# A four-layer decoder trunk on one core: q and k computed transposed, rotated by a partition shuffle, and scored two heads at a time

## The chip, the cores and the metric

The kernel runs on one core of a Trainium2 chip. The metric is the device time of one execution in microseconds, the median of several runs. The core has a matrix engine (TensorE, PE in the profile; its weight loads are PEld), a vector engine (VectorE, DVE), an activation engine (ScalarE, ACT), a general engine (GpSimd, POOL) and a queue for DMAs (SyncE, SP).

## The reference

The input is one sequence of 256 tokens with 1024 features in fp32. Four layers follow each other. Each has a token mixer and a SwiGLU FFN (1024 to 2 x 2816 to 1024), and after each of the two `x <- LN(alpha * x + f(x))`. The mixers are causal attention with heads of 64; the first 16 dims of each head of q and k are rotated by position (dims 0 to 7 with 8 to 15).

- Layers 0 and 3: 16 query heads, 4 key and value heads, a window of 128 keys, a learned sink per head in the softmax, biases on q, k, v and the output.
- Layer 1: three groups of q, k, v with windows and strides (128, 1), (512, 4) and (2048, 16), 16 heads each. The groups' outputs are merged by their softmax denominators, which is one softmax over all three groups' keys.
- Layer 2: block-sparse attention with blocks of 256. With 256 tokens no past block exists, so it is causal attention within the block, 16 heads.

```python
def apply_rope(x, cos, sin):                       # x1, x2: dims 0-7 and 8-15 of each head
    return concatenate([x1 * c - x2 * s, x2 * c + x1 * s, x[..., 16:]])
s = einsum('bnqhgd,bnkhd->bnhgqk', qb, kb) * dh ** -0.5   # masked, softmax, times v
x = layer_norm(DN_ALPHA * x + mixer(x), ln_g[i, 0], ln_b[i, 0])
x = layer_norm(DN_ALPHA * x + swiglu(x), ln_g[i, 1], ln_b[i, 1])
```

## The kernel before

**Numbers in two parts.** Every fp32 operand of a product is kept as two fp16 parts, high and low. `mm3` (L127 to L132) issues three matmuls for one product: high x high (L130), high x low (L131), low x high (L132). Weights come from DRAM in fp32, in chunks of 1024 x 512 (128 partitions x 8 k-tiles x 512 columns). `load_w` casts each chunk in pieces of 1024 columns: ACT writes the high part `whi` (L91), DVE the low part `wlo` (L92). Four chunks fit in SBUF at a time, so casts run ahead of their use by that much. `split` (L134 to L139) makes the two parts of an activation: ACT the high one (L135), DVE the low one (L137 or L139).

**Projections.** `proj` (L178) computes 128 tokens x 512 columns of `x @ w` with the transposed activations `xth`, `xtl` as the stationary operand and the weights moving, 24 matmuls of 512 columns. For q and k the result has tokens on partitions. It is copied to the tile `qkv` (by ACT at L520, or with its bias by DVE at L455), rotated in place on POOL by four instructions on the 16 rotated dims of each head (L197 to L200, `rope`), transposed by PE with four fp32 transposes of 128 x 128 (L206), and split into `qkh`, `qkl` (L135, L137). Those hold two heads on the 128 partitions, 64 dims each. The transposes wait in a list `late` and are issued 8 projection steps later, or earlier where `flush` asks for them. For layers 0 and 3 the 4 key heads are first copied twice side by side (L466), so that a key head lies on the same 64 partitions as each query head that uses it.

**Attention.** `attend` (L212) makes steps for a list of items. An item is one query tile of 128 tokens with two heads (layers 0, 2, 3) or one head and its three key groups (layer 1). The step `scores` issues `mm3` on 64 partitions per head and key group, takes mask and row maximum on DVE straight from PSUM (L252) and the exponential with its row sum on ACT (L255). `flip` transposes the probabilities on PE (L268) and splits them, `values` multiplies by v into the tile `pv`, `collect` transposes the normalised output (L299). They are issued 0, 2, 3 and 4 items later. PSUM has 8 banks: three accumulators `acc`, four tiles `at` for scores and transposes, one `pv`.

**Order.** `weave` issues the attention steps of one set of heads evenly between the projection steps of the next set; `finish` does the same with the output projection of the heads that are done, and ends with the layer norm. The framework then puts the instructions in order at build time, by the program's order and by its own estimate of when operands are ready, so the order on an engine can differ from the program's. It also writes all waits. Each engine works through its queue in order.

Of the kernel before, what the change touches and what calls it, by code (L numbers as in the profile page):

```python
# [32 lines left out]
# Weights are scaled by a power of two before they are split into two fp16  # L33
# parts, so that the low part stays in fp16's normal range.
# [9 lines left out]
def trunk(ctx, tc, a, out):  # L44
# [16 lines left out]
    cc = const.tile([P, NT, ROT], F32, name="cc")  # L61
    ss = const.tile([P, NT, ROT], F32, name="ss")
    h8 = ROT // 2
# [32 lines left out]
    def weight_list():  # L96
        for li in range(DEPTH):
            kind, j = li % 3, li // 3
            if kind == 0:
                for c in (2, 0, 1):  # L100
                    yield a["w_a"][j, c], 8
                wo_ = a["w_ao"][j]
            else:
                m, wo_ = (a["w_b"], a["w_bo"][0]) if kind == 1 else (a["w_c"], a["w_co"][0])
                for c in range(m.shape[0]):
                    yield m[c], 8
            for h in range(2):
                yield wo_[h], 8
            for c in range(NFB // 2):
                yield a["w_gu"][li, c], 8  # L110
            for h in range(2):
                for c, n in enumerate((8, 8, 6)):
                    yield a["w_dn"][li, h, :, 4096 * c:4096 * c + 512 * n], n
# [30 lines left out]
    def weave(main, fill):  # L144
        """issue two lists of steps, evenly interleaved"""
# [9 lines left out]
    def transpose_x(t, XT, half):  # L155
        """columns of X[t] (512 of them) -> XT, in two parts"""
# [10 lines left out]
    late, age = [], [0]  # L167

    def flush(keys=None):
        """issue the transposes that wait: all, or those up to the last that writes one of keys"""  # L170
        while late and (keys is None or any(e[1] in keys for e in late)):
            late.pop(0)[2]()

    def proj(XT, w, t, evac):
        """steps for [128 tokens, 512] = x @ w for a chunk of 512 columns"""
        cell = {}

        def k_step(k):  # L178
            if k == 0:
                cell["ps"] = acc.tile([P, 512], F32, name="acc")  # L180
            mm3(cell["ps"], sl2(XT, ALL, k, tok(t)), sl2(w, ALL, k), k == 0, k == NK - 1)
            age[0] += 1
            while late and age[0] - late[0][0] >= LAG:
                late.pop(0)[2]()
            if k == NK - 1:
                evac(cell["ps"], t)
        return [lambda k=k: k_step(k) for k in range(NK)]

    def rope(y, t, nh):
        """y [128, nh, 64] fp32, in place"""  # L190
        t1 = sm.tile([P, nh, ROT], F32, name="rope1", bufs=2)
        t2 = sm.tile([P, nh, ROT], F32, name="rope2", bufs=2)
        cb = cc[:, t:t + 1, :].to_broadcast([P, nh, ROT])
        sb0 = ss[:, t:t + 1, :h8].to_broadcast([P, nh, h8])
        sb1 = ss[:, t:t + 1, h8:].to_broadcast([P, nh, h8])
        e = nc.gpsimd
        e.tensor_tensor(t1, y[:, :, :ROT], cb, op=OP.mult)  # L197
        e.tensor_tensor(t2[:, :, :h8], y[:, :, h8:ROT], sb0, op=OP.mult)
        e.tensor_tensor(t2[:, :, h8:], y[:, :, :h8], sb1, op=OP.mult)
        e.tensor_tensor(y[:, :, :ROT], t1, t2, op=OP.add)  # L200

    def transpose_qk(y, t, dst):
        """y [128 tokens, 4 pairs of heads x 128] -> dst parts [128, 4, 256 tokens]"""
        ps = ats.tile([P, 4, P], F32, name="at")
        for j in range(4):
            nc.tensor.transpose(ps[:, j], y[:, j * P:(j + 1) * P], ident)  # L206
        split(dst[0][:, :, tok(t)], dst[1][:, :, tok(t)], ps)
# [4 lines left out]
    def attend(items, oT):  # L212
        """steps for softmax attention. items: (query tile, heads, keys of their transposes), with heads [(head, groups, sinks)]
        and groups [(qT, kT, v)]: qT, kT parts [64, 256], v parts [128, NT, 64]; sinks [128, heads]
        (negated) or None. The groups' keys share one softmax. Four heads in a row, of one query tile,
        make a quad, whose outputs are normalised and transposed together."""
        st, quads = {}, {}

        def quad(i):
            t, heads = items[i][:2]  # L220
            return quads.setdefault((t, heads[0][0] // 4), {})

        def scores(i):
            t, heads = items[i][:2]
            flush([(k, tt) for k in items[i][2] for tt in range(t + 1)])
            nk, ng, nh = (t + 1) * P, len(heads[0][1]), len(heads)
            per, n = 512 // nk, nk * ng
            sk, mk = heads[0][2], MASK[heads[0][3]][t]
# [3 lines left out]
            s = sm.tile([P, 768], F32, name="s", bufs=4)  # L232
            s = s[:, :nh * (n + (sk is not None))].rearrange("p (h n) -> p h n", h=nh)
            if sk is not None:
                nc.gpsimd.tensor_copy(s[:, :, n], sk)
            mn = sm.tile([P, 4], F32, name="mn", bufs=6)
            ps = None
            for hi, (h, groups, _, _) in enumerate(heads):
                m = None
                for g, (qT, kT, _) in enumerate(groups):  # L240
                    u = hi * ng + g
                    if u % per == 0:
                        ps = ats.tile([P, 512], F32, name="at")
                    o = u % per * nk
                    mm3(ps[:, o:o + nk], sl2(qT, ALL, tok(t)), sl2(kT, ALL, slice(0, nk)), True, True)
                    if u % per == per - 1 or g == ng - 1:
                        # the groups of this head in this bank
                        g0 = max(0, g - u % per)
                        c0, c1 = g0 * nk, (g + 1) * nk
                        init = (3e38 if sk is None else sk[:, hi:hi + 1]) if m is None else m  # L250
                        m = mn[:, 2 * hi + (g0 > 0):2 * hi + (g0 > 0) + 1]
                        nc.vector.tensor_tensor_reduce(  # L252
                            s[:, hi, c0:c1], ps[:, o + nk - (c1 - c0):o + nk], mk[:, c0:c1], scale=-QSC,
                            scalar=init, op0=OP.add, op1=OP.min, accum_out=m)
                nc.scalar.activation(s[:, hi], s[:, hi], AF.Exp, bias=m, scale=-1.0,  # L255
                                     accum_out=q["l"][:, h % 4:h % 4 + 1])
            st[i] = s

        def flip(i):
            t, heads = items[i][:2]  # L260
            nq = len(heads[0][1]) * (t + 1)
            nb = len(heads) * nq
            s, parts = st[i], []
            for b0 in range(0, nb, 4):
                bn = min(4, nb - b0)
                ps = ats.tile([P, 4, P], F32, name="at")
                for b in range(bn):
                    nc.tensor.transpose(ps[:, b], s[:, (b0 + b) // nq, tok((b0 + b) % nq)], ident)  # L268
# [6 lines left out]
        def values(i):  # L275
            t, heads = items[i][:2]
# [4 lines left out]
            for h, groups, _, _ in heads:  # L281
                nb = len(groups) * (t + 1)
                for b in range(nb):
                    g, kt = divmod(b, t + 1)
                    mm3(q["o"][:, h % 4], parts.pop(0), sl2(groups[g][2], ALL, kt), b == 0, b == nb - 1)
            if h % 4 == 3:
# [4 lines left out]
        def collect(i):  # L291
            t, heads = items[i][:2]
            h, q = heads[-1][0], quad(i)
            if h % 4 != 3:
                return
# [4 lines left out]
            pr = slice(h // 4 * 2, h // 4 * 2 + 2)  # L300
            split(oT[0][:, pr, tok(t)], oT[1][:, pr, tok(t)], ps)
# [8 lines left out]
    def halves(tq, pr, hh):  # L310
        return sl2(tq, slice(hh * DH, (hh + 1) * DH), pr)
# [43 lines left out]
    def out_steps(PS, lhs, nk, w, h, t, ks, k0=0):  # L355
        """steps of PS[h, t] += lhs.T @ w over the k-tiles ks (of w's, w starting at k0)"""
# [67 lines left out]
    def finish(li, oT, items, kA, folded=False):  # L424
        """the last heads' attention, beside the output projection of the others, and LN"""
# [6 lines left out]
        f0 = o(0, range(kA))  # L432
        weave(attend(i0, oT), f0[:5] + [flush] + f0[5:])
# [8 lines left out]
    def mixer_a(li, j, XT):  # L442
        bias = hbuf("hth")[:, :1536]
# [4 lines left out]
        vv = (big.tile([P, NT, 4, DH], F16, name="avh"), big.tile([P, NT, 4, DH], F16, name="avl"))  # L448
# [3 lines left out]
        def evac(c):  # L452
            def fn(ps, t):
                y = two.tile([P, 512], F32, name="qkv", bufs=3)
                nc.vector.scalar_tensor_tensor(y, ps, 1.0 / WS, bias[:, 512 * c:512 * c + 512],  # L455
                                               op0=OP.mult, op1=OP.add)
                yh = y.rearrange("p (h d) -> p h d", d=DH)
                if c < 2:
                    rope(yh, t, 8)
# [260 lines left out]
```

## Time and profile before

| | |
|---|---|
| Time, median of 3 runs | 1289.69 us (1289.64 to 1290.55) |
| Span of the profiled execution | 1288.2 us; its own time is not given beside the span |
| PE busy | 1265.8 us |
| DVE busy | 873.0 us |
| ACT busy | 664.0 us |
| POOL busy | 112.7 us |
| DMA | 233.31 MB, mean 181 GB/s |
| Granted TensorE clock, mean | 0.997 of full |

A span runs from the first to the last instruction of one execution. "Busy" is the time in which at least one instruction of an engine was under way. Matmuls overlap in their pipeline, so the duration of one is longer than the distance to the next; that distance, read from a timeline of starts, is what a matmul costs in a full queue. In a timeline, consecutive instructions of one line and kind are merged into one row, with their count behind an x.

### The profile page before, as it was taken

What the parts mean: (1) busy time and instruction counts of PE and PEld (TensorE: products, weight loads), DVE (VectorE), ACT (ScalarE), POOL (GpSimd) and SP (SyncE); (2) the same over time, 40 slices, a digit from 0 to 9 for tenths busy, and PEclk for the clock granted to TensorE, in tenths of its full rate; (3) what the DMA queues carried; (4) which work ended last, traced back from release to release, by engine and by line L of the source; (5) the groups of instructions that cost most, each with busy time, mean ns of one, the idle gap of its engine ahead of it and who ended that gap; (6) DMA issues with size and microseconds to landing.
All of it is one profiled execution on the core that took longest, in us unless ns stands there. A gap on an engine that the chain in (4) does not pass through costs nothing. (4 is left out here: it accounts for less than half of the span.)

```text
span 1288.2 us, 24678 instructions
## 1 busy us (share of the span) xinstructions
PE 1265.8 (98%) x10352; PEld 844.9 (66%) x10352; DVE 873.0 (68%) x1451; ACT 664.0 (52%) x1117; POOL 112.7 (9%) x230
## 2 busy tenths in 40 slices
PE   7989999999999999999999999999999999999997
PEld 3549988444555555589884445589884445898843
DVE  5888766475565666777665667777665687876652
ACT  5765654345555565446544456536544366464430
POOL 1410000012011101000000020100000041000000
PEclk9999999999999999999999999999999999999999
DMA  8445755656345334347555564247555552475520
GB/s 316 166 164 197 263 200 184 221 206 222 145 147 173 139 131 151 112 163 251 209 181 180 201 225 162 100 164 257 203 180 182 223 207 99 153 250 207 190 87 33
DMA packets 35663, 233.31 MB, mean 181 GB/s; under 512 B 4448, under 2 KB 4448, under 8 KB 9696
## 3 DMA queue, kind: packets, MB, share of 16 engines
q1 hardware_dynamic: 35552, 231.74, 51.0%
q8 instruction: 81, 1.33, 0.4%
q14 instruction: 30, 0.25, 0.1%
HBM read 230.68 MB, written 1.05 MB: 180 GB/s over the span
## 5 line engine op out<-in xcount | busy, mean ns | idle before, releaser
L92 DVE SCALAR_TENSOR_TENSOR wlo<-raw,whi 128x1024 f16<-128x1024 f32 x416 | 500.3, 1223 | 206.1 <-ACT whi L91 205.8
L91 ACT ACTIVATE whi<-raw 128x1024 f16<-128x1024 f32 x416 | 414.6, 1049 | 258.9 <-PE acc L132 92.1
L131 PE MATMUL acc<-xtl,whi 128*128 128x256 f16 (+1 forms) x1792 | 408.2, 250 | 0.0
L132 PE MATMUL acc<-xth,wlo 128*128 128x256 f16 (+1 forms) x1792 | 408.2, 250 | 0.0
L130 PE MATMUL acc<-xth,whi 128*128 128x256 f16 (+1 forms) x1792 | 408.0, 250 | 0.1
L130 PE MATMUL acc<-whi,xth 128*128 128x512 f16 x480 | 183.3, 382 | 2.4 <-ACT xth L135 2.4
L131 PEld LDWEIGHTS <-whi 128*128 128x128 f16 x1792 | 175.3, 98 | 12.5 <-issue 0.3
L130 PEld LDWEIGHTS <-whi 128*128 128x128 f16 x1792 | 175.3, 98 | 11.9
L131 PE MATMUL acc<-wlo,xth 128*128 128x512 f16 x480 | 183.0, 381 | 0.2 <-DVE wlo L92 0.2
L132 PE MATMUL acc<-whi,xtl 128*128 128x512 f16 x480 | 182.8, 381 | 0.3
L132 PEld LDWEIGHTS <-wlo 128*128 128x128 f16 x1792 | 175.3, 98 | 11.6
L130 PE MATMUL acc<-whi,hth 128*128 128x512 f16 x352 | 133.4, 379 | 0.0
L131 PE MATMUL acc<-wlo,hth 128*128 128x512 f16 x352 | 133.4, 379 | 0.0
L132 PE MATMUL acc<-whi,htl 128*128 128x512 f16 x352 | 133.4, 379 | 0.0
L255 ACT ACTIVATE s<-s,mn 128x257 f32<-128x257 f32 (+5 forms) x128 | 67.6, 529 | 46.3 <-DVE mn L252 46.1
L333 POOL TENSOR_TENSOR mv<-mv,nhalf 128x1 f32<-128x1 f32 x16 | 15.8, 986 | 817.5 <-DVE mv L332 817.5
L132 PEld LDWEIGHTS <-xtl 128*128 128x128 f16 x480 | 47.3, 99 | 57.8 <-DVE xtl L137 3.0
L130 PEld LDWEIGHTS <-xth 128*128 128x128 f16 x480 | 47.2, 98 | 48.4 <-issue 5.0
L135 ACT ACTIVATE hth<-hf 128x256 f16<-128x256 f32 x88 | 36.5, 415 | 74.5 <-DVE hf L377 74.5
L131 PEld LDWEIGHTS <-xth 128*128 128x128 f16 x480 | 47.2, 98 | 40.3 <-issue 1.5
L137 DVE TENSOR_TENSOR pl<-at,ph 128x512 f16<-128x512 f32 (+2 forms) x96 | 51.5, 551 | 19.0 <-ACT ph L135 18.5
L132 PEld LDWEIGHTS <-htl 128*128 128x128 f16 x352 | 34.4, 98 | 41.5
(93 smaller groups left out, 1499.0 us busy)
## 6 DMA issues: line engine op xcount, KB each, us to landing
raw<-in_w_gu SPq DMA_DIRECT2D x88, 1024.0 KB, 4.9
raw<-in_w_dn SPq DMA_DIRECT2D x40, 1024.0 KB, 4.9
raw<-in_w_b SPq DMA_DIRECT2D x36, 1024.0 KB, 5.0
raw<-in_w_c SPq DMA_DIRECT2D x12, 1024.0 KB, 4.9
raw<-in_w_a SPq DMA_DIRECT2D x10, 1024.0 KB, 5.5
raw<-in_w_ao SPq DMA_DIRECT2D x8, 1024.0 KB, 6.0
gb<-in_ln_g SPq DMA_DIRECT2D x8, 512.0 KB, 4.6
gb<-in_ln_b SPq DMA_DIRECT2D x8, 512.0 KB, 5.9
```

The costliest lines, as they stand in the source:

```text
L91: nc.scalar.activation(hi[:, c + d:c + e], r[:, d:e], AF.Copy, scale=WS)
L92: nc.vector.scalar_tensor_tensor(lo[:, c + d:c + e], r[:, d:e], WS, hi[:, c + d:c + e], op0=OP.mult, op1=OP.subtract)
L130: nc.tensor.matmul(ps, st[0], mv[0], start=start, stop=False)
L131: nc.tensor.matmul(ps, st[0], mv[1], start=False, stop=False)
L132: nc.tensor.matmul(ps, st[1], mv[0], start=False, stop=stop)
L135: nc.scalar.activation(hi, src, AF.Copy, scale=1.0 if scale is None else scale)
L137: nc.vector.tensor_tensor(lo, src, hi, op=OP.subtract)
L255: nc.scalar.activation(s[:, hi], s[:, hi], AF.Exp, bias=m, scale=-1.0, accum_out=q["l"][:, h % 4:h % 4 + 1])
L333: nc.gpsimd.tensor_tensor(mv[:, 3:4], mv[:, 2:3], nhalf, op=OP.pow)
```

## The change

- q and k are projected transposed. `proj_t` makes the weights stationary (128 columns at a time, two heads) and lets the transposed activations move, over 128 or 256 tokens. The result has two heads' dims on the partitions and tokens along the free axis. The fp32 transposes, the list `late` and the copies of k are gone.
- The rotation works on that layout. `rope_t` copies the result out on ACT (with the bias, which is now one number per partition), swaps partitions 0 to 7 with 8 to 15 of each group of 32 by a DVE stream shuffle, and does two multiplications and an addition on POOL over the whole tile, with tables of cos and sin on all partitions (1 and 0 where nothing is rotated). Then it splits.
- For layers 0 and 3 the columns of q (and the rows of the output projection, the sinks, the biases) are put in another order on loading, so that the two query heads of a pair use the two key heads of a pair, and k is kept once. The first chunk is k and v together.
- An item of attention is now one or two pairs of heads. The two heads of a pair lie on the two halves of the partitions; their matmuls are issued in turn, into two PSUM tiles. Steps follow 0, 1, 2 and 3 items later.

```diff
-    LAG, LF, LV, LO = 8, 2, 3, 4
+    LF, LV, LO = 1, 2, 3
...
+    def proj_t(XT, w, js, ts, evac, per=2):
+        cell, todo = {}, [(j, k) for j in js for k in range(NK)]
+        def step(part):
+            for j, k in part:
+                if (j, k) == todo[0]:
+                    ps = acc.tile([P, 512], F32, name="acc")
+                    cell["ps"] = ps[:, :len(js) * (ts.stop - ts.start)].rearrange("p (j n) -> p j n", j=len(js))
+                mm3(cell["ps"][:, j - js[0]], sl2(w, ALL, k, slice(j * P, (j + 1) * P)), sl2(XT, ALL, k, ts),
+                    k == 0, k == NK - 1)
+                if (j, k) == todo[-1]:
+                    evac(cell["ps"], js, ts)
+        return [lambda i=i: step(todo[i:i + per]) for i in range(0, len(todo), per)]
+
+    swap = [(i ^ 8) if i < ROT else i for i in range(32)]
+
+    def rope_t(ps, dst, ts, bias=None):
+        nj, n = ps.shape[1], ts.stop - ts.start
+        y = two.tile([P, 512], F32, name="qkv")[:, :nj * n].rearrange("p (j n) -> p j n", j=nj)
+        z = two.tile([P, 512], F32, name="qkz")[:, :nj * n].rearrange("p (j n) -> p j n", j=nj)
+        if bias is None:
+            nc.scalar.activation(y, ps, AF.Copy, scale=1.0 / WS)
+        else:
+            for j in range(nj):
+                nc.scalar.activation(y[:, j], ps[:, j], AF.Identity, bias=bias[:, j:j + 1], scale=1.0 / WS)
+        nc.vector.stream_shuffle(z.rearrange("p j n -> p (j n)"), y.rearrange("p j n -> p (j n)"), swap)
+        table = lambda c: c[:, ts].unsqueeze(1).to_broadcast([P, nj, n])
+        nc.gpsimd.tensor_tensor(z, z, table(ss), op=OP.mult)
+        nc.gpsimd.tensor_tensor(y, y, table(cc), op=OP.mult)
+        nc.gpsimd.tensor_tensor(y, y, z, op=OP.add)
+        split(dst[0], dst[1], y)
...
         def scores(i):
-            for hi, (h, groups, _, _) in enumerate(heads):
-                for g, (qT, kT, _) in enumerate(groups):
-                    if u % per == 0:
-                        ps = ats.tile([P, 512], F32, name="at")
-                    mm3(ps[:, o:o + nk], sl2(qT, ALL, tok(t)), sl2(kT, ALL, slice(0, nk)), True, True)
+            units = [(pi, g) for pi in range(len(pairs)) for g in range(ng)]
+            for u0 in range(0, len(units), per):
+                bank = units[u0:u0 + per]
+                ps = [ats.tile([P, 512], F32, name="at") for _ in range(2)]
+                for b, (pi, g) in enumerate(bank):
+                    qT, kT, _ = pairs[pi][1][g]
+                    for st_, mv in ((0, 0), (0, 1), (1, 0)):
+                        for hh in range(2):
+                            r = slice(hh * DH, (hh + 1) * DH)
+                            nc.tensor.matmul(ps[hh][:, b * nk:(b + 1) * nk], qT[st_][r, tok(t)], kT[mv][r, 0:nk],
+                                             start=(st_, mv) == (0, 0), stop=st_ == 1)
...
     def mixer_a(li, j, XT):
+        pk = [proj_t(XT, wk, (0, 1), tok(t), evac(kT, 0), 4) + proj(XT, wk, t, evac_v, slice(256, 512))
+              for t in range(NT)]
+        p0 = [proj_t(XT, w0, (0, 1, 2, 3), tok(t), evac(qTs[0], 2), 4) for t in range(NT)]
         if li == 0:
-            weave(pk[0], pk[1])
-            run(p0[0] + p0[1])
+            run(pk[0] + pk[1] + p0[0] + p0[1])
...
     def mixer_bc(li, XT, ng):
         def evac_qk(g, quad):
-            def fn(ps, t):
-                y = two.tile([P, 512], F32, name="qkv", bufs=3)
-                nc.scalar.activation(y, ps, AF.Copy, scale=1.0 / WS)
-                rope(y.rearrange("p (h d) -> p h d", d=DH), t, 8)
-                late.append((age[0], ((g, quad), t), lambda: transpose_qk(y, t, qk)))
+            def fn(ps, js, ts):
+                rope_t(ps, sl2(qk, ALL, slice(js[0], js[-1] + 1), ts), ts)
+        def chunk_steps(w, qk, ev):
+            if qk:
+                return [f for js in ((0, 1), (2, 3)) for f in proj_t(XT, w, js, slice(0, SEQ), ev)]
+            return proj(XT, w, 0, ev) + proj(XT, w, 1, ev)
...
+    ang, trn = rows("qkv"), rows("qkv")
+    nc.vector.tensor_copy(ang, pos_i)
+    nc.vector.tensor_scalar(ang, ang, inv, None, op0=OP.mult)
...
+    nc.scalar.activation(ss, ang, AF.Sin)
+    nc.scalar.activation(cc, ang, AF.Sin, scale=0.5)
```

## Rows read from the trace of the kernel before

**Rows 1.** Page, busy time of each engine (share of the span) and its instructions.

```profile
PE 1265.8 (98%) x10352; PEld 844.9 (66%) x10352; DVE 873.0 (68%) x1451; ACT 664.0 (52%) x1117; POOL 112.7 (9%) x230
```

**Rows 2.** Waits of PE: engine, line, for whom: us in total, times, longest us.

```profile
PE at L206 <- POOL qkv L200: 1.6, 2, 1.2
PE at L206 <- ACT qkv L466: 1.3, 2, 1.0
```

**Rows 3.** Windows, the mixers of layers 0 to 3 from first projection to FFN.

```profile
core 0: us, PE busy (x) PEld busy (x) DVE busy (x) ACT busy (x) POOL busy (x), PEclk, DMA share, GB/s
10.45:102.47 92.02, 86.72 (x576) 45.30 (x577) 80.31 (x182) 61.48 (x137) 21.64 (x41) 0.98 0.57 203
277.21:557.98 280.77, 280.61 (x1953) 155.47 (x1952) 183.40 (x307) 156.65 (x262) 40.28 (x98) 1.00 0.43 154
733.01:847.53 114.52, 114.05 (x738) 58.86 (x737) 80.76 (x171) 65.18 (x142) 18.61 (x38) 1.00 0.45 156
1022.26:1106.67 84.41, 82.14 (x585) 43.54 (x584) 69.99 (x164) 48.88 (x122) 22.55 (x38) 1.00 0.42 153
```

**Rows 4.** PE's timeline in layer 0, one visit to half rows (64*128): start, us.

```profile
42.30 0.38 PE L132 MATMUL acc<-whi,xtl 128*128 128x512 f16 x1
42.61 0.23 PE L130 MATMUL at<-qkh,qkh 64*128 64x128 f16 x1
42.67 0.22 PE L131 MATMUL at<-qkl,qkh 64*128 64x128 f16 x1
42.73 0.22 PE L132 MATMUL at<-qkh,qkl 64*128 64x128 f16 x1
42.88 0.39 PE L130 MATMUL acc<-whi,xth 128*128 128x512 f16 x1
```

**Rows 5.** PE's timeline, transposes of q; and the chain of waits, eight others.

```profile
37.21 0.66 PE L206 MATMUL at<-ident,qkv 128*128 128x128 f32 x4 [1.22 <-POOL qkv L200]
37.71 0.38 PE L130 MATMUL acc<-whi,xth 128*128 128x512 f16 x1
...
1104.02 0.87 PE at L160 x8
```

**Rows 6.** PE's timeline, two heads in turn, 256 columns (layer 0) and 128 (layer 3).

```profile
82.58 0.29 PE L130 MATMUL at<-qkh,qkh 64*128 64x256 f16 x2
82.70 0.28 PE L131 MATMUL at<-qkl,qkh 64*128 64x256 f16 x2
82.81 0.28 PE L132 MATMUL at<-qkh,qkl 64*128 64x256 f16 x2
...
1051.68 0.24 PE L130 MATMUL at<-qkh,qkh 64*128 64x128 f16 x2
1051.75 0.23 PE L131 MATMUL at<-qkl,qkh 64*128 64x128 f16 x2
```

**Rows 7.** PE's timeline in the FFN, first and last of eleven and of eight.

```profile
102.81 0.22 PE L130 MATMUL acc<-xth,whi 128*128 128x128 f16 x1
...
103.37 0.22 PE L131 MATMUL acc<-xtl,whi 128*128 128x128 f16 x1
...
149.81 0.27 PE L132 MATMUL acc<-xth,wlo 128*128 128x256 f16 x1
...
150.58 0.27 PE L130 MATMUL acc<-xth,whi 128*128 128x256 f16 x1
```

**Rows 8.** PE's timeline, starts of the first and the last visit to half rows.

```profile
39.31 0.23 PE L130 MATMUL at<-qkh,qkh 64*128 64x128 f16 x1
...
1092.43 0.28 PE L130 MATMUL at<-qkh,qkh 64*128 64x256 f16 x1
```

**Rows 9.** Lines by duration (ns min/median/max, first and last start us): POOL, DVE.

```profile
L200 POOL TENSOR_TENSOR qkv<-rope,rope x44: 317/455/1569, 27.5 to 1073.9; 128x128 f32<-128x128 f32 x40, 128x64 f32<-128x64 f32 x4
...
L198 POOL TENSOR_TENSOR rope<-qkv,ss x44: 247/319/1416, 25.8 to 1072.2; 128x64 f32<-128x64 f32 x40, 128x32 f32<-128x32 f32 x4
...
L92 DVE SCALAR_TENSOR_TENSOR wlo<-raw,whi x416: 1170/1220/1480, 9.9 to 1247.9; 128x1024 f16<-128x1024 f32 x139
```

**Rows 10.** Groups by form: count | busy us, mean ns | idle before, released by.

```profile
L137 DVE TENSOR_TENSOR qkl<-at,qkh 128x512 f16<-128x512 f32 x44 | 30.2, 686 | 29.0 <-ACT qkh L135 28.9
```

**Rows 11.** ACT's timeline at the start: the fourth piece of the first weights.

```profile
15.68 1.06 ACT L91 ACTIVATE whi<-raw 128x1024 f16<-128x1024 f32 x1 [1.93 <-DMA raw<-in_w_a]
```

More of the change, by code (lines that the diff above doesn't have):

```diff
@@ L99, in weight_list @@
             if kind == 0:
-                for c in (2, 0, 1):
+                for c in range(3):
                     yield a["w_a"][j, c], 8
@@ L165, in new_xt, with proj @@
         return (big.tile([P, NK, SEQ], F16, name="xth"), big.tile([P, NK, SEQ], F16, name="xtl"))
[L167 to L174, printed above, removed]
+    def proj(XT, w, t, evac, cols=slice(0, 512)):
         cell = {}
@@ L180, in k_step @@
                 cell["ps"] = acc.tile([P, 512], F32, name="acc")
[L181 to L184, printed above, removed]
+            mm3(cell["ps"][:, cols], sl2(XT, ALL, k, tok(t)), sl2(w, ALL, k, cols), k == 0, k == NK - 1)
             if k == NK - 1:
-                evac(cell["ps"], t)
+                evac(cell["ps"][:, cols], t)
         return [lambda k=k: k_step(k) for k in range(NK)]
[L189 to L200, printed above, removed]
@@ L219, in quad @@
         def quad(i):
-            t, heads = items[i][:2]
-            return quads.setdefault((t, heads[0][0] // 4), {})
+            t, pairs = items[i]
+            return quads.setdefault((t, pairs[0][0] // 2), {})
         def scores(i):
-            t, heads = items[i][:2]
-            flush([(k, tt) for k in items[i][2] for tt in range(t + 1)])
-            nk, ng, nh = (t + 1) * P, len(heads[0][1]), len(heads)
+            t, pairs = items[i]
+            nk, ng = (t + 1) * P, len(pairs[0][1])
             per, n = 512 // nk, nk * ng
-            sk, mk = heads[0][2], MASK[heads[0][3]][t]
+            sk, mk = pairs[0][2], MASK[pairs[0][3]][t]
             q = quad(i)
@@ L231, in scores @@
                 q["l"] = sm.tile([P, 4], F32, name="l", bufs=6)
-            s = sm.tile([P, 768], F32, name="s", bufs=4)
-            s = s[:, :nh * (n + (sk is not None))].rearrange("p (h n) -> p h n", h=nh)
+            s = [sm.tile([P, 768], F32, name="s")[:, :len(pairs) * (n + (sk is not None))].rearrange(
+                "p (h n) -> p h n", h=len(pairs)) for _ in range(2)]
             if sk is not None:
-                nc.gpsimd.tensor_copy(s[:, :, n], sk)
-            mn = sm.tile([P, 4], F32, name="mn", bufs=6)
@@ L237, in scores @@
-            ps = None
-            for hi, (h, groups, _, _) in enumerate(heads):
-                m = None
-                for g, (qT, kT, _) in enumerate(groups):
-                    u = hi * ng + g
-                    if u % per == 0:
-                        ps = ats.tile([P, 512], F32, name="at")
-                    o = u % per * nk
-                    mm3(ps[:, o:o + nk], sl2(qT, ALL, tok(t)), sl2(kT, ALL, slice(0, nk)), True, True)
[L246 to L251, printed above, removed]
-                        nc.vector.tensor_tensor_reduce(
[L253 to L256, printed above, removed]
+                for pi, pair in enumerate(pairs):
+                    for hh in range(2):
+                        nc.gpsimd.tensor_copy(s[hh][:, pi, n:n + 1], pair[2][:, hh:hh + 1])
@@ L257, in scores @@
             st[i] = s
         def flip(i):
-            t, heads = items[i][:2]
-            nq = len(heads[0][1]) * (t + 1)
-            nb = len(heads) * nq
+            t, pairs = items[i]
+            n = len(pairs[0][1]) * (t + 1)
+            nb = 2 * len(pairs) * n
             s, parts = st[i], []
@@ L275, in values @@
         def values(i):
-            t, heads = items[i][:2]
+            t, pairs = items[i]
             q, parts = quad(i), st.pop(i)
@@ L280, in values @@
                 turn[0] = 1 - turn[0]
[L281 to L286, printed above, removed]
+            for pr, groups, _, _ in pairs:
+                for hh in range(2):
+                    nb = len(groups) * (t + 1)
+                    for b in range(nb):
+                        g, kt = divmod(b, t + 1)
+                        mm3(q["o"][:, (2 * pr + hh) % 4], parts.pop(0), sl2(groups[g][2][hh], ALL, kt), b == 0,
+                            b == nb - 1)
+            if pr % 2 == 1:
                 nc.vector.reciprocal(q["l"], q["l"])
@@ L291, in collect @@
         def collect(i):
-            t, heads = items[i][:2]
-            h, q = heads[-1][0], quad(i)
-            if h % 4 != 3:
+            t, pairs = items[i]
+            pr, q = pairs[-1][0], quad(i)
+            if pr % 2 == 0:
                 return
@@ L442, in mixer_a @@
     def mixer_a(li, j, XT):
-        bias = hbuf("hth")[:, :1536]
+        vbias = hbuf("hth")[:, :256]
+        tbias = two.tile([P, 10], F32, name="tbias", bufs=1)
         bo = hbuf("htl")[:, :D]
@@ L473, in items @@
             for t in range(NT):
-                for pr in range(4):
-                    heads = []
-                    for hh in range(2):
-                        h = 8 * c + 2 * pr + hh
-                        g = h // 4
-                        heads.append((h, [(halves(qTs[c], pr, hh), halves(kT, g, hh), sl2(vv, ALL, ALL, g))],
-                                      nsink[:, h - hh:h - hh + 2], 0))
-                    out.append((t, heads, (c, 2)))
+                for q in range(2):
+                    pairs = []
+                    for pr in (2 * q, 2 * q + 1):
+                        groups = [(sl2(qTs[c], ALL, pr), sl2(kT, ALL, c),
+                                   [sl2(vv, ALL, ALL, 2 * c + hh) for hh in range(2)])]
+                        h = 8 * c + 2 * pr
+                        pairs.append((4 * c + pr, groups, nsink[:, h:h + 2], 0))
+                    out.append((t, pairs))
             return out
@@ L559, in items @@
             for t in range(NT):
+                pairs = []
                 for pr in range(2):
-                    heads = []
-                    for hh in range(2):
-                        gl = []
-                        for g in range(ng):
-                            v, off = vs[g, quad]
-                            qk = qks[g, quad]
-                            gl.append((halves(qk, pr, hh), halves(qk, 2 + pr, hh),
-                                       sl2(v, ALL, ALL, off + 2 * pr + hh)))
-                        heads.append((4 * quad + 2 * pr + hh, gl, None, 1 if ng == 1 else 2))
-                    for hs in ([heads] if ng == 1 else [heads[:1], heads[1:]]):
-                        out.append((t, hs, [(g, quad) for g in range(ng)]))
+                    gl = []
+                    for g in range(ng):
+                        v, off = vs[g, quad]
+                        qk = qks[g, quad]
+                        gl.append((sl2(qk, ALL, pr), sl2(qk, ALL, 2 + pr),
+                                   [sl2(v, ALL, ALL, off + 2 * pr + hh) for hh in range(2)]))
+                    pairs.append((2 * quad + pr, gl, None, 1 if ng == 1 else 2))
+                out += [(t, ps) for ps in ([pairs] if ng == 1 else [pairs[:1], pairs[1:]])]
             return out
@@ L581, in mixer_bc @@
                 run(p)
-        for ev in first[2:]:
-            wc = next_w()
-            for t in range(NT):
-                run(proj(XT, wc, t, ev))
+        for c in first[2:]:
+            run(chunk_steps(next_w(), *c))
         if ng == 1:
@@ L681, in _lay @@
             ccols += [qkv(2, q), qkv(2, q + 1)]
+    heads = [8 * c + 4 * hh + p for c in range(2) for p in range(4) for hh in range(2)]
+    hcols = np.concatenate([A(h * DH, (h + 1) * DH) for h in heads])
+    acols = np.concatenate([A(1024, 1536), hcols])
+    ab = np.asarray(i["a_b_qkv"])
+    inv = (np.float32(THETA) ** (-np.arange(0, ROT, 2, dtype=np.float32) / np.float32(ROT))).astype(np.float32)
+    inv = np.concatenate([-inv, inv, np.zeros(DH - ROT, np.float32)])
     gu = []
@@ L700, in _lay @@
         "masks": _masks(),
[L701 removed]
+        "inv": np.tile(inv, 2)[:, None],
     }
```

125 lines of the change are left out of this document (57 added, 68 removed).

## The prediction

> **What bounds the kernel now.** I read the page's busy shares first: TensorE (PE) is busy 98% of the span, VectorE (DVE) 68%, ScalarE (ACT) 52%, GpSimd (POOL) 9% [rows 1]. A busy PE need not be a working one, so next came PE's own timeline, for the distance from one matmul's start to the next. Nearly everywhere it equals the columns that pass: 0.22 us for 512 columns, 0.11 for 256, 0.056 for 128 [rows 4, 7]. So PE is the bound, and what leaves its queue shortens the kernel until another engine is late. Third, the windows of the four token mixers: PE fills 86.7 of 92.0 us in layer 0, 280.6 of 280.8 in layer 1, 114.1 of 114.5 in layer 2 and 82.1 of 84.4 in layer 3 [rows 3]. DVE fills 87%, 65%, 71% and 83% of the same stretches: the reader is to see that layers 0 and 3 have little behind PE. The FFNs between them are not touched.
>
> **What PE loses and gains.**
>
> *Transposes.* The 176 fp32 transposes of q and k go (12 + 4 + 2 x 3 chunks of 512 columns, two token tiles each, four transposes in each). Eight transposes issue in 0.87 us, or 0.109 each; four after a pause take 0.50 us, from 37.21 to 37.71 [rows 5]. That is 19.2 to 22.0 us; I take 20.
>
> *Scores.* There are 576 half-row matmuls, half with 128 columns and half with 256. Alone they follow each other at 0.056 us (42.67 to 42.73 [rows 4]) and 0.11. What two of them cost on opposite row halves can be seen already, because at a few places the kernel before issues two heads in turn: three times x2 start at 82.58, 82.70, 82.81, so a pair of 256 columns costs about 0.11 us, and the x2 of 128 columns at 1051.68 and 1051.75 about 0.06 [rows 6]. The pair costs what one costs. Before: 288 x 0.109 + 288 x 0.056 = 47.5 us; after, half: 23.8 saved. The bounds are 0 (no overlap) and 23.8; I take 23.8, since the rows show just this order.
>
> *Changes between full and half rows.* The last full matmul before half-row ones takes 0.31 us instead of 0.22 (42.30 to 42.61), the last half-row one 0.15 instead of 0.06 (42.73 to 42.88). From 42.30 to 42.88 it is 0.58 us for 0.216 + 3 x 0.056 = 0.38 us of columns: 0.20 per visit [rows 4]. The timeline has 111 visits, the first at 39.31, the last at 1092.43 [rows 8], though the program has 80 items; the order of issue splits some. After, the program has 40 items (two heads each in layer 1, four elsewhere). 40 to 56 visits save 14.2 to 11; I take 12.
>
> *Narrower matmuls.* With the weights stationary, a chunk over 256 tokens is 96 matmuls of 256 columns instead of 48 of 512: 96 x 0.109 - 48 x 0.216 = 0.1 us more; over 128 tokens at a time 192 of 128 columns, 192 x 0.056 - 10.37 = 0.4 more. The FFN shows that weight loads stay hidden at both widths: ten starts in 0.56 us, seven in 0.77 [rows 7]. Three chunks are of the second kind in layers 1 and 2, one and the k half in each of layers 0 and 3: 3.8 us in all, with 3 and 5 as ends.
>
> Together 20 + 23.8 + 12 - 3.8 = 52.0 us off PE. By heads and chunks: 8.4 in each of layers 0 and 3, 25.9 in layer 1, 9.3 in layer 2. PE then wants 83.6, 254.9, 105.2 and 76.0 us of the four mixers.
>
> **What stands behind PE.**
>
> *Shuffle.* DVE gets one per evacuation: 40 of 512 columns and 4 of 256. No row shows one. The nearest is a DVE pass over as many elements, 686 ns [rows 10]; twice that is the upper end, and a gain is excluded since nothing like it was there. I take 0.68: 16.3 us in layer 1, 5.4 in layer 2, 3.5 in layers 0 and 3, where the bias pass shrinks from six of 512 columns to two of 256 (-3.3; q's and k's bias moves to ACT, which is free for 30 us of layer 0 and 35 of layer 3 [rows 3]). The split's subtraction keeps its count. The tables of cos and sin, now 256 wide, add some 2 us to layer 0. DVE: 82.5, 199.7, 86.2, 70.2.
>
> *Rotation on POOL.* Three passes over 512 columns replace four over 64 to 128. The medians 455 ns (128 columns) and 319 (64) give 2.1 ns a column [rows 9], so 1.27 us each as an estimate; the ends are 0.69 (DVE's speed) and 2.3 (five times the 128-column median). Over 40 evacuations that is 152 us on an engine with 113 of 1288 used: hidden, 3.8 us per evacuation, while PE makes the next half chunk in 48 x 0.109 = 5.2 us.
>
> *The two engines hold each other up.* A POOL pass took up to 1569 ns against 455, a DVE cast of weights up to 1480 against 1220 [rows 9]. DVE lost at most 0.26 us at a time to passes of 0.3 to 0.5. Passes of 1.27 us can cost it 0 to 1.27 each; I take 0.2 (12 + 6 short passes in layers 0 and 3, 72 in layer 1, 24 in layer 2): DVE then wants 86, 214, 91 and 74 us. Against PE's wishes that is 103%, 84%, 86% and 97%. Layer 0 falls short by 2.4 at least; casts of the FFN's weights can be put off into the FFN, about one chunk (4 x 1.22 us), but the queue is in order and the scores' maximum waits behind a cast. I take 4 us lost in layer 0, 2 in layer 3, 2 and 1 in layers 1 and 2.
> The Trainium skill (SBUF — State Buffer, "Who interferes with whom") states that a DVE instruction with two SBUF inputs and a GpSimd instruction that reads SBUF exclude each other for the whole instruction. Taken at its hardest, with each pass finding a DVE instruction waiting, that is the slower rival below; the rows agree that there is a wait, but have it short.
>
> *Longer way from projection to scores.* Copy, shuffle, three POOL passes, two split passes: 3.8 + 4 x 0.69 = 6.5 us if a pass of ACT takes what DVE's does, behind whatever ACT and DVE have queued, and ACT's split stands in order before the weight casts and the exponentials. In layer 1 the value chunks (10 us each) hide it. It shows where a q chunk ends just ahead of its scores: twice in each of layers 0 and 3, once in layer 2; 0 to 5 us at each. PE's present waits for the rotated columns (1.6 us for POOL's last pass, 1.3 for ACT's copy of k [rows 2]) go. Net +1.5.
>
> *Start.* The first product now runs all eight k-tiles for 128 columns before the next columns, and the fourth piece of the first weights is cast only from 15.68 us on [rows 11]. In program order PE would sit from about 12 to 18 us; products of the same chunk whose pieces are there can fill in. 0 to 6; I take 2.
>
> *At nothing.* Score tiles: two or four of the four PSUM tiles are taken at once; in layer 1 four to five fill steps of 0.65 us stand between two attention steps, enough for one pass of DVE; without that cover it would be about 1 us for each of 8 items. Sink copies go from 32 to 64 short ones on POOL, ahead of the exponential only. DMAs: one more small one per mixer of layers 0 and 3 on SP's queue, a smaller bias broadcast before it; the weights' order stays.
>
> Sum: 52.0 - (4 + 2 + 2 + 1) - 1.5 - 2 = 39.5. The page gives the profiled execution only as its span, 1288.2 us; the median of the three runs is 1.5 more, which I carry: 1288.2 - 39.5 + 1.5 = **1250 us**, with its own range 1243 to 1258.
>
> **Rivals.**
>
> *All of it (25%).* DVE's casts move out of the way and PE stays saturated: 1289.7 - 52 = 1238, range 1230 to 1243. For it: the page shows PE full with DVE at 83% in layer 3. Against: the sums for layers 0 and 3.
>
> *The evacuating engines become the bound (15%).* Halved scores come faster than DVE and ACT take maxima, exponentials and splits; layers 0 and 3 gain nothing, 1 and 2 half: 35.2 / 2 - 2 = 15.6 less, 1274. For it: where DVE is at 83 to 87%, PE idles 2.3 and 5.3 us, at 65% only 0.2 [rows 3]. Against: layer 1 has half the gain and most room.
> The Trainium skill's TensorEngine Tiling page ("PSUM Bottleneck") has this as a rule: tiling speeds the matmuls, not the evacuation, which may become the bottleneck. No row before shows it, as nearly all scores came one at a time.
>
> *No overlap (4%).* The order of issue breaks the pairs: 23.8 us lost again, 1274. Against: rows 6.
>
> *POOL blocks DVE (6%), slower.* The place is the three rotation passes. If each holds a waiting DVE instruction for all its 1.27 us, DVE wants 102.1, 291.1, 116.7 and 89.8 us of stages that took 92.0, 280.8, 114.5 and 84.4: +28 us, 1318. It decides from about 1.05 us of loss per pass (438.6 + 126.8 x = 571.7). Against: the greatest loss was 0.26.
>
> **Chances.** Forecast 50%, the others as given. Faster by over 0.2% 94%, within 0.2% (2.6 us, about what a measurement can tell) 2%, slower 4%: the last rival with a third of it near no change. The range 1233 to 1270 holds the forecast, most of the first rival and the better part of the second.
>
> **What would show it.** Right: no transpose of qkv; half-row matmuls in x2 steps of 0.06 and 0.11; 40 to 56 visits; PE still 96% or more; layer 1 some 24 us shorter, layer 0 only 3 to 5. Wrong: POOL passes well over 1.3 us with casts lengthened by a microsecond (last rival); PE waits on DVE's maximum or ACT's exponential inside layer 1 (second); visits above 80, which takes away 6 us or more; a first matmul group that waits for casts beyond 18 us.

## The result, and the profile after

The changed kernel takes 1383.7 us (median of 4 runs, 1381.0 to 1385.0) against 1289.7: a ratio of 1.0725, interval 1.071 to 1.074. It is 94 us slower, where 40 us less was forecast.

The page's busy shares and the windows of the four mixers, each from its first projection to its FFN, answer to [rows 1] and [rows 3].

```profile
PE 1260.9 (91%) x11808; PEld 940.7 (68%) x11808; DVE 918.3 (66%) x1507; ACT 664.2 (48%) x1121; POOL 236.8 (17%) x218
```

```profile
core 0: us, PE busy (x) PEld busy (x) DVE busy (x) ACT busy (x) POOL busy (x), PEclk, DMA share, GB/s
10.34:115.68 105.34, 82.86 (x840) 59.55 (x840) 85.31 (x182) 63.83 (x145) 34.35 (x51) 0.92 0.53 178
290.42:616.68 326.26, 280.39 (x2625) 203.69 (x2624) 213.10 (x347) 154.17 (x254) 118.14 (x74) 0.93 0.40 133
791.42:929.93 138.51, 116.73 (x993) 78.45 (x992) 87.49 (x183) 64.04 (x138) 42.69 (x34) 0.91 0.39 129
1104.66:1201.19 96.53, 78.44 (x849) 57.44 (x848) 74.08 (x168) 50.37 (x130) 32.01 (x44) 0.93 0.37 127
```

Every mixer became longer, by 13.3, 45.5, 24.0 and 12.1 us, 95 together, layer 1 most of all, where DVE had the most room [rows 3]. No engine is full: PE idles 1382.6 - 1260.9 = 121.7 us of its span, before 22.4. PE's clock, before at 1.00 outside layer 0's start, is at 0.91 to 0.93 of full.

What was taken off PE did go. Its timeline in layer 1, two heads in turn, answers to [rows 6]:

```profile
454.19 0.27 PE L131 MATMUL acc<-xth,wlo 128*128 128x256 f16 x1
454.39 0.28 PE L252 MATMUL at<-qkh 64*128 64x256 f16 x2
454.51 0.27 PE L252 MATMUL at<-qkl,qkh 64*128 64x256 f16 x2
454.62 0.27 PE L252 MATMUL at<-qkh,qkl 64*128 64x256 f16 x2
...
455.28 0.27 PE L252 MATMUL at<-qkh,qkl 64*128 64x256 f16 x2
455.48 0.28 PE L129 MATMUL acc<-xth,whi 128*128 128x256 f16 x1
```

From the first pair of 256 columns at 454.39 to the ninth at 455.28 it is 0.89 us, 0.11 a pair. The whole timeline has 44 visits to half rows, before 111, and no transpose of q or k. The time is lost in waits (engine, line, for whom: us in total, times, longest us):

```profile
ACT qkh L134 <- POOL qkv L209: 190.5, 44, 6.8
DVE qkl L136 <- ACT qkh L134: 122.3, 42, 4.6
...
PE at L281 <- DVE mn L262: 25.0, 8, 7.1
PE at L252 <- ACT qkh L134: 24.2, 6, 7.2
PE at L314 <- DVE oy L304: 16.5, 8, 3.7
```

L134 and L136 are the two passes of the split; L209 is the last POOL pass. ACT stood 190 us before POOL and DVE 122 us before ACT. PE's three longest lines make 65.7 of its 121.7 idle us. At L252 a score waits for the split of its own q (three times in layer 0, once in layer 2, twice in layer 3). At L281 and L314 PE waits for a row maximum or a normalised output of the attention, which DVE reaches late. The longest wait of PE inside layer 1 shows what stood behind them. First DVE, then POOL, ACT and PE, all around 458 to 469 us, but for two earlier exponentials of ACT (L267):

```profile
458.49 0.72 DVE L205 STREAM_SHUFFLE qkz<-qkv 128x512 f32<-128x512 f32 x1
459.10 1.21 DVE L91 SCALAR_TENSOR_TENSOR wlo<-raw,whi 128x1024 f16<-128x1024 f32 x1
464.68 0.69 DVE L136 TENSOR_TENSOR qkl<-qkv,qkh 128x512 f16<-128x512 f32 x1 [4.37 <-ACT qkh L134]
465.29 0.68 DVE L262 CUSTOM_DVE_ANT_0 s<-at,masks 128x512 f32<-128x512 f32 x1
```

```profile
459.28 2.15 POOL L207 TENSOR_TENSOR qkz<-qkz,ss 128x512 f32<-128x512 f32 x1 [2.93 <-DVE qkz L205]
461.39 1.26 POOL L208 TENSOR_TENSOR qkv<-qkv,cc 128x512 f32<-128x512 f32 x1
462.73 1.26 POOL L209 TENSOR_TENSOR qkv<-qkv,qkz 128x512 f32<-128x512 f32 x1
```

```profile
447.39 0.94 ACT L267 ACTIVATE s<-s,mn 128x768 f32<-128x768 f32 x1 [1.50 <-DVE mn L262]
...
448.32 0.92 ACT L267 ACTIVATE s<-s,mn 128x768 f32<-128x768 f32 x1
...
457.87 0.58 ACT L201 ACTIVATE qkv<-acc 128x512 f32<-128x512 f32 x1
464.02 0.63 ACT L134 ACTIVATE qkh<-qkv 128x512 f16<-128x512 f32 x1 [5.57 <-POOL qkv L209]
```

```profile
458.66 0.27 PE L131 MATMUL acc<-xth,wlo 128*128 128x256 f16 x1
466.03 2.82 PE L281 MATMUL at<-ident,s 128*128 128x128 f32 x12 [7.10 <-DVE mn L262]
468.65 0.42 PE L129 MATMUL acc<-xth,whi 128*128 128x256 f16 x1
468.86 0.42 PE L130 MATMUL acc<-xtl,whi 128*128 128x256 f16 x1
```

The scores left PE by 455.5. Their maximum (L262) could have run then, but in DVE's queue it stands behind the second split pass of another chunk (L136), which waits for ACT's first, which waits for three POOL passes. From 460.3 to 464.7 DVE does nothing, ACT nothing from 458.5 to 464.0, and PE stands for 7.1 us.

What PE stands before are the twelve transposes of the item before this one (L281). Their probabilities were ready at 449.2, when ACT's two exponentials ended (the next one starts at 467.0), so it is not their data that they wait for. They need PSUM tiles `at`, and an item of layer 1 with 256 keys per group now puts its scores into all four of them; the first comes free when its maximum has been taken, at 466.0. So the late maximum stops PE through the score tiles. After the wait the same 256 columns take 0.21 us instead of 0.11: PE has dropped from the 2.4 to the 1.2 GHz level. The window behind the wait shows it (PEclk 0.50), and the one from 474 shows it back:

```profile
454.00:458.70 4.70, 4.70 (x53) 3.82 (x50) 2.14 (x4) 2.06 (x3) 2.27 (x2) 1.00 0.69 227
466.00:470.00 4.00, 3.97 (x19) 3.50 (x20) 2.08 (x9) 2.97 (x6) 0.00 (x0) 0.50 0.00 0
470.00:474.00 4.00, 4.00 (x45) 3.35 (x44) 3.63 (x4) 2.32 (x4) 3.62 (x3) 0.83 0.00 0
474.00:478.00 4.00, 4.00 (x39) 3.59 (x37) 2.19 (x3) 2.85 (x4) 1.11 (x1) 1.00 0.00 0
```

### The profile page after: what moved, and what is told of

The parts are those of the page before. It is cut to its first block, busy times and chain, and to the rows that moved or that the text cites. A ratio compares the mean times of both kernels' runs of the same rounds, so it can differ in the third digit from the quotient of the medians.

```text
span 1382.6 us, 27545 instructions
## 1 busy us (share of the span) xinstructions
PE 1260.9 (91%) x11808; PEld 940.7 (68%) x11808; DVE 918.3 (66%) x1507; ACT 664.2 (48%) x1121; POOL 236.8 (17%) x218
## 3 DMA queue, kind: packets, MB, share of 16 engines
HBM read 229.50 MB, written 1.05 MB: 167 GB/s over the span
## 5 line engine op out<-in xcount | busy, mean ns | idle before, releaser
L91 DVE SCALAR_TENSOR_TENSOR wlo<-raw,whi 128x1024 f16<-128x1024 f32 x416 | 527.7, 1286 | 205.1 <-ACT whi L90 204.5
L130 PE MATMUL acc<-xtl,whi 128*128 128x256 f16 (+1 forms) x2656 | 613.9, 252 | 8.5 <-DVE xtl L136 8.5
L129 PE MATMUL acc<-xth,whi 128*128 128x256 f16 (+1 forms) x2656 | 614.5, 253 | 5.1 <-ACT xth L134 5.1
L131 PE MATMUL acc<-xth,wlo 128*128 128x256 f16 (+1 forms) x2656 | 613.7, 252 | 1.3 <-DVE wlo L91 1.2
L131 PEld LDWEIGHTS <-wlo 128*128 128x128 f16 x2656 | 263.3, 99 | 30.6 <-issue 9.9
L129 PEld LDWEIGHTS <-whi 128*128 128x128 f16 x2656 | 263.6, 99 | 25.0 <-issue 2.5
L130 PEld LDWEIGHTS <-whi 128*128 128x128 f16 x2656 | 263.3, 99 | 23.5 <-issue 4.2
L134 ACT ACTIVATE qkh<-qkv 128x512 f16<-128x512 f32 (+1 forms) x48 | 28.5, 594 | 193.9 <-POOL qkv L209 190.5
L136 DVE TENSOR_TENSOR qkl<-qkv,qkh 128x512 f16<-128x512 f32 (+1 forms) x48 | 32.6, 680 | 122.3 <-ACT qkh L134 122.3
L207 POOL TENSOR_TENSOR qkz<-qkz,ss 128x512 f32<-128x512 f32 (+1 forms) x44 | 66.6, 1515 | 273.9 <-DVE qkz L205 273.8
L281 PE MATMUL at<-ident,s 128*128 128x128 f32 x288 | 52.1, 310 | 31.8 <-DVE mn L262 25.0
L267 ACT ACTIVATE s<-s,mn 128x257 f32<-128x257 f32 (+5 forms) x128 | 66.9, 525 | 26.3 <-DVE mn L262 26.2
L208 POOL TENSOR_TENSOR qkv<-qkv,cc 128x512 f32<-128x512 f32 (+1 forms) x44 | 79.5, 1807 | 0.0
L134 ACT ACTIVATE hth<-hf 128x256 f16<-128x256 f32 x88 | 36.5, 415 | 73.9 <-DVE hf L388 73.9
L129 PE MATMUL acc<-whi,xth 128*128 128x512 f16 (+1 forms) x160 | 62.4, 390 | 8.8 <-DVE htl L138 5.0
L281 PEld LDWEIGHTS at<-ident,s 128*128 128x128 f32 x288 | 37.4, 156 | 44.0 <-ACT s L267 17.8
L209 POOL TENSOR_TENSOR qkv<-qkv,qkz 128x512 f32<-128x512 f32 (+1 forms) x44 | 63.3, 1440 | 3.4
```

Source lines behind the costliest of these rows:

```text
L91: nc.vector.scalar_tensor_tensor(lo[:, c + d:c + e], r[:, d:e], WS, hi[:, c + d:c + e], op0=OP.mult, op1=OP.subtract)
L129: nc.tensor.matmul(ps, st[0], mv[0], start=start, stop=False)
L130: nc.tensor.matmul(ps, st[0], mv[1], start=False, stop=False)
L131: nc.tensor.matmul(ps, st[1], mv[0], start=False, stop=stop)
L134: nc.scalar.activation(hi, src, AF.Copy, scale=1.0 if scale is None else scale)
L136: nc.vector.tensor_tensor(lo, src, hi, op=OP.subtract)
```

## The experiments

Three theories stood after this reading. *Queue:* the split's place in the in-order queues of ACT and DVE, ahead of the attention's maxima and exponentials, makes POOL's latency everyone's. *Port:* POOL's long passes and DVE's casts shut each other out, as in the prediction's last rival. *Attention:* the new items (two heads, shorter lags, all four score tiles) starve PE by themselves.

**No rotation at all** (`e1_norot`): q and k are left unrotated.

```diff
-        nc.vector.stream_shuffle(z..., y..., swap)
...
-        nc.gpsimd.tensor_tensor(z, z, table(ss), op=OP.mult)
-        nc.gpsimd.tensor_tensor(y, y, table(cc), op=OP.mult)
-        nc.gpsimd.tensor_tensor(y, y, z, op=OP.add)
         split(dst[0], dst[1], y)
```

> The changed kernel with the rotation of q and k left out: no shuffle and no POOL passes, the split takes the copy of the projection. Queue theory (the split of q and k stands in ACT's and DVE's in-order queues and waits there for POOL's three passes, and the maxima and exponentials behind it come late): the 190 us that ACT and the 122 us that DVE wait there go, and what was taken off PE shows: 1240 us (1230 to 1255). Port theory (POOL's passes and DVE's casts exclude each other): the same 1240. Attention theory (pairs, shorter lags and four score tiles leave PE waiting, whatever the rotation does): 1330 or more.

1246.8 us, 0.968 of before (0.966 to 0.970). The rotation costs the changed kernel 137 us, and without it the attention keeps PE as full as before. The attention theory falls as a cause by itself; the four score tiles matter only once the maxima are late (PE waits 2.9 us for maxima here, 25.0 in the changed kernel).

```profile
PE 1217.1 (98%) x11808; PEld 921.2 (74%) x11808; DVE 858.3 (69%) x1419; ACT 664.1 (53%) x1121; POOL 29.2 (2%) x86
```

Against the changed kernel PE is busy 1260.9 - 1217.1 = 43.8 us less for the same 11808 matmuls, and idle 121.7 - 28.3 = 93.4 less. The granted clock is 0.995 in the mean here and 0.962 in the changed kernel, so most of the 43.8 are matmuls at the lower level.

**Passes that nobody reads** (`e6_nowait`): shuffle and passes stay, but the split takes the unrotated copy.

```diff
-        nc.gpsimd.tensor_tensor(y, y, table(cc), op=OP.mult)
-        nc.gpsimd.tensor_tensor(y, y, z, op=OP.add)
+        nc.gpsimd.tensor_tensor(z, y, table(cc), op=OP.mult)
+        nc.gpsimd.tensor_tensor(z, y, z, op=OP.add)
         split(dst[0], dst[1], y)
```

> The changed kernel with the shuffle and POOL's three passes of the same size, but into a tile that nobody reads: the split takes the copy of the projection, so q and k stay unrotated. Queue theory: nothing waits for POOL, so within 15 us of the kernel without the passes, 1240 to 1260. Port theory: POOL holds the port as long as in the changed kernel, so 1350 to 1385. Attention theory: 1350 or more.

1285.4 us, 0.996 of before (0.995 to 0.997). It lies in no theory's range, between that of the queue and that of the port: to wait for the passes costs 1383.7 - 1285.4 = 98 us, to have shuffle and passes run costs 39 more.

**The shuffle without the passes** (`e8_shuffle`), its result unread:

```diff
         nc.vector.stream_shuffle(z..., y..., swap)
...
-        nc.gpsimd.tensor_tensor(z, z, table(ss), op=OP.mult)
-        nc.gpsimd.tensor_tensor(y, y, table(cc), op=OP.mult)
-        nc.gpsimd.tensor_tensor(y, y, z, op=OP.add)
```

> The changed kernel with the shuffle but no POOL passes, and the shuffle's result read by nobody (q and k unrotated). Between the kernel without any rotation (1247 us) and the one with unread passes (1285 us) lie 39 us. Port theory for these 39: they are DVE's lost time beside POOL, so with the passes gone 1250 us (1245 to 1258). Load theory: they are the 30 us of shuffles on DVE, 1270 us or more.

1250.2 us, 0.970 of before (0.968 to 0.972). Of the 39 the shuffle is 3, the POOL passes 35. How they cost it shows in the cast of weights (group of L91, mean ns of one behind the busy time), first with the unread passes, then without:

```profile
L91 DVE SCALAR_TENSOR_TENSOR wlo<-raw,whi 128x1024 f16<-128x1024 f32 x416 | 549.6, 1340 | 206.1 <-ACT whi L90 205.5
```

```profile
L91 DVE SCALAR_TENSOR_TENSOR wlo<-raw,whi 128x1024 f16<-128x1024 f32 x416 | 498.4, 1217 | 214.6 <-ACT whi L90 214.1
```

The same 416 casts take 51 us longer; DVE as a whole is busy 956.0 against 882.4 us, 74 more, though it does the same work. Of the other 23 the second pass of the split has 20; with unread passes it runs beside them (mean 1065 against 636 ns). That the unread passes hold the buffers of `qkv` and `qkz` longer is not what costs: ACT and DVE wait 3.2 us for POOL there.

**The attention alone** (`e2_pairs`): projection, rotation and PE transposes of the kernel before, with the new items, pairs in turn and short lags.

```diff
-    LAG, LF, LV, LO = 8, 2, 3, 4
+    LAG, LF, LV, LO = 8, 1, 2, 3
...
-                    mm3(ps[:, o:o + nk], sl2(qT, ALL, tok(t)), sl2(kT, ALL, slice(0, nk)), True, True)
+                    for st_, mv in ((0, 0), (0, 1), (1, 0)):
+                        for hh in range(2):
+                            r = slice(hh * DH, (hh + 1) * DH)
+                            nc.tensor.matmul(ps[hh][:, b * nk:(b + 1) * nk], qT[st_][r, tok(t)], kT[mv][r, 0:nk],
+                                             start=(st_, mv) == (0, 0), stop=st_ == 1)
```

> The kernel before (projection with tokens on partitions, rotation of 16 dims on POOL, PE transposes) with the new attention alone: pairs issued in turn, lags 0, 1, 2, 3. Queue and port theories: the score and visit terms show, 1289.7 - 23.8 - 12 = 1254 us (1245 to 1268). Attention theory: PE waits as in the changed kernel, 1310 or more.

1266.1 us, 0.983 of before (0.981 to 0.984), with the attention's part of the change alone. It is the fastest version here that leaves nothing out. PE is busy 32.5 us less (1265.8 to 1233.3; 23.8 + 12 were predicted), and 7.8 of them return as idle time. PE waits 0.4 us for maxima, with the same four score tiles.

```profile
PE 1233.3 (98%) x10352; PEld 829.1 (66%) x10352; DVE 866.4 (69%) x1431; ACT 656.6 (52%) x1097; POOL 125.3 (10%) x262
```

**The passes on DVE** (`e3_dve_rot`):

```diff
-        nc.gpsimd.tensor_tensor(z, z, table(ss), op=OP.mult)
+        nc.vector.tensor_tensor(z, z, table(ss), op=OP.mult)
```

and so for the other two.

> The changed kernel with the three rotation passes on DVE instead of POOL, behind the shuffle on the same engine. Queue theory: ACT's wait falls from about 4.3 us a time to 2.8 us or less and DVE waits for nothing between shuffle and third pass, but DVE gets 130 passes of 0.69 us: 1285 us (1255 to 1320). Port theory: no POOL pass is left, DVE only 90 us busier: 1260 (1245 to 1290). Attention theory: 1380 or more.

1284.7 us, 0.997 of before (0.996 to 0.999). On the busier engine the rotation costs 99 us less than on the idle one. The ranges of the queue and of the port theory both hold this time, so this run does not tell them apart. ACT's wait for the last pass is 78 us instead of 190, and DVE waits 3.5 us for ACT there instead of 122.

**The same passes on POOL, the split later in the queue** (`e5_defer`): only the order on ACT and DVE differs.

```diff
+    def flush(behind, keys=None):
+        """issue the splits that wait (all, or up to the last with one of keys), queued behind these instructions"""
+        while late and (keys is None or any(e[0] in keys for e in late)):
+            _, dst, y = late.pop(0)
+            with ExitStack() as order:
+                for i in behind:
+                    order.enter_context(tc.issue_after(i))
+                split(dst[0], dst[1], y)
...
+        flush(last(ACT, DVE))
...
-        split(dst[0], dst[1], y)
+        late.append((key, dst, y))
...
+            flush(mark[0], items[i][2])
```

`last` gives the instructions issued last on the two engines. `flush` is called behind the next evacuation's shuffle or value chunk, and before the scores that read the chunk.

> The changed kernel with its whole rotation, but the two split passes of a half chunk are queued, by order edges alone, behind the next evacuation's copy on ACT and shuffle on DVE (or behind the scores issued last), half a chunk of PE's work (5.2 us) later. Queue theory: neither engine stands before POOL's passes any more, so it comes to the kernel whose passes nobody reads (1285 us) plus what is exposed where scores follow their chunk at once: 1295 us (1275 to 1315). If the waits in the two queues were not the cause, no change from 1384 (1365 or more).

1305.8 us, 1.013 of before (1.011 to 1.016). The order alone gives back 78 of the 98 us. The waits that remain:

```profile
ACT qkh L134 <- POOL qkv L226: 87.3, 32, 7.9
...
DVE qkl L136 <- ACT qkh L134: 28.7, 14, 4.0
```

Half a chunk is not always enough. PE itself stands 19.3 us at five scores that wait for the split of their own q, against 0.4 with the unread passes. A still later place was not tried.

**One pass on POOL, two on DVE, split late** (`e11_share`):

```diff
+                nc.vector.tensor_tensor(y, y, z, op=OP.add)
+                split(dst[0], dst[1], y)
...
         nc.gpsimd.tensor_tensor(z, z, table(ss), op=OP.mult)
-        nc.gpsimd.tensor_tensor(y, y, table(cc), op=OP.mult)
-        nc.gpsimd.tensor_tensor(y, y, z, op=OP.add)
-        split(dst[0], dst[1], y)
+        if bias is None:
+            nc.vector.scalar_tensor_tensor(y, ps, 1.0 / WS, table(cc), op0=OP.mult, op1=OP.mult)
+        else:
+            nc.vector.tensor_tensor(y, y, table(cc), op=OP.mult)
+        flush(last(ACT, DVE))
+        late.append((key, dst, y, z))
```

The first two lines stand in `flush`.

> The deferred version with one POOL pass instead of three: the product with cos is taken by DVE straight from PSUM (one SBUF operand), the sum by DVE ahead of the deferred split. DVE gets 80 passes of 0.69 us more, and POOL holds the port 40 times instead of 120. Queue and port theories together: DVE loses 67 / 3 = 22 us instead of 67 and works 55 more, so about 10 us better or equal to the deferred version, 1280 us (1265 to 1300). If only the queue mattered: slower than the deferred version by 10 to 30 us.

1283.3 us, 0.995 of before (0.993 to 0.997). It is 22 us faster than the late split with three POOL passes, though DVE has 88 passes more (80 of full size). Casts are back at a mean of 1218 ns, and DVE is busy only 954.9 against 943.4 us. But the way to the split is shorter too: PE's waits for the split of its own q fall from 19.3 to 7.2 us. So the run does not show how much of the 22 us is the port's.

## Why the prediction was wrong, point by point

The forecast put 94% on a faster kernel, and its one slower rival reached 1318 us.

- *Transposes, scores, visits, narrower matmuls: right.* Without the rotation PE's busy time fell by 1265.8 - 1217.1 = 48.7 us; 52.0 were predicted. Pairs cost what one matmul costs, visits went to 44 (40 to 56 said).
- *Longer way from projection to scores: the step that failed.* The prediction worked out 6.5 us, noted that ACT's split stands ahead of casts and exponentials, and then priced only the five places where a score waits for its own q: +1.5 us net. Even there it was too low: PE stood 24.2 us at six such places. And it left out what is queued behind the split at all 44 evacuations: late maxima and normalised outputs held PE another 25.0 and 16.5 us (2.9 and 0.6 without the rotation). The wait cost 98 us, shown by taking it away with the passes left in place (98) and by moving the split in the queue alone (78 of them). The 98 are not clear of the port: the three passes waited for take 4.8 us by their means and 3.8 alone.
- *Score tiles, put at nothing: wrong together with that wait.* The prediction had about 1 us for each of 8 items without cover. PE stood 25.0 us in 8 waits for maxima, the longest of them, 7.1 us, for the tiles that they free. By themselves the four tiles cost little: 0.4 us with the attention alone.
- *POOL's passes: sized well alone, badly together.* 1.27 us estimated, 1.26 measured alone, but 2.1 to 2.3 beside a DVE cast; means of the 44 passes are 1.44 to 1.81.
- *The two engines hold each other up: mis-sized in time.* 0.2 us lost per pass was taken, and 9 us of time for all that DVE gets. Beside the unread passes DVE lost 74 us over 132 passes, 0.56 each, which cost 35 us of time. In the changed kernel itself it was busy 918.3 - 882.4 = 35.9 us more than without the passes, 0.27 each; there a split waits for its own passes and cannot run beside them. The 0.2 was read from the longest cast before (1480 ns), beside passes of a third of the length. On the rival's scale (decides from 1.05) the larger loss is halfway: the rival by itself did not come true, and DVE at 65% of layer 1 was not the bound [rows 3].
- *Shuffle: right.* 0.70 us each, and 3 us of time.
- *Start: right within its ends.* In the first 32 us PE stood 6.7 us behind splits, a cast and the first value chunk, before 2.4; 2 us were taken, 0 to 6 said.
- *Evacuating engines as the bound:* not the cause; with pairs and without the rotation PE is 98% busy.
- *What the sum left out:* idle PE at these lengths also loses its clock. Matmuls behind the waits ran at half rate; that is most of the 44 us that PE is busy longer than without the rotation.
- *What remains open:* the last 20 us between the late split (1305.8) and the unread passes (1285.4). The 19.3 us that PE still stands at scores fit, and stand at the five places that the prediction named (twice in layers 0 and 3, once in layer 2), but no run takes that wait away with the rotation kept. How the 137 us of the rotation divide between waiting and port can depend on which is taken away first; the runs took the wait away first.

The Trainium skill's rule of mutual exclusion (SBUF — State Buffer, "Who interferes with whom") held in kind: the blocked instruction's duration grew, up to 2309 ns for a cast. At its hardest it would have cost every pass in full, 1.27 us; these runs show 0.27 and 0.56.

## What to carry to other kernels

An idle engine is not free if its result is consumed by an instruction in a busy engine's in-order queue: price a new hop between engines at up to its latency times the number of times that another stream's work stands behind the waiting instruction (here 190 us of waiting, of which 98 cost time), and look in the queue for who that is. Ask also which buffers that late work holds, here the score tiles. Put the consumer late in its queue, or the step on one of the consumer's own engines, even if that engine is busier. Before making a pass four times as wide to save instructions, check what it shuts out while it runs.

## What the runs showed of the hardware

- A POOL product of 128 x 512 fp32 takes 1.26 us alone and up to 2.36 beside DVE; a DVE stream shuffle of the same size 0.73.
- Two half-row matmuls on opposite halves, in two PSUM tiles, start 3 ns apart in the median and cost what one costs, 0.11 us a pair of 256 columns over 18 matmuls in a row.
- Behind 7.1 us without a matmul PE was granted half its clock (0.50 in the stretch from 466), and the full one again in the stretch from 474, after matmuls without a pause.
